# A sliding-window copy from DRAM to DRAM: row by row in 64 KB packets, or in four orders of addresses

## The chip, the cores and the metric

One core of one Trainium2 chip runs the kernel. The metric is the device time of one launch in microseconds (us), lower is better. Before the change the median of two runs is 819.74 us (819.61 and 819.86).

## What is computed

The input `x` has 32 batches of 4096 rows of 256 float32 values. A window is 64 rows and starts every 32 rows, so each batch has 127 windows, and every window is copied out whole:

```python
def reference(x, window_size, stride):          # 64, 32
    batch, length, dim = x.shape                # 32, 4096, 256
    n_windows = (length - window_size) // stride + 1        # 127
    result = np.zeros((batch, n_windows, window_size, dim), dtype=np.float32)
    for i in range(n_windows):
        start = i * stride
        result[:, i] = x[:, start:start + window_size].copy()
    return result
```

A window is 64 x 256 x 4 = 65,536 bytes, contiguous in the input and in the output. Two neighbouring windows share half of their input. Below, a "block" is half a window: 32 rows, 32 KB. A batch of the input is 128 blocks (4 MiB, exactly 2^22 bytes); every block but the first and the last of a batch stands in the output twice, as the second half of one window and as the first half of the next. The output has 32 x 127 = 4064 windows, 266.34 MB.

## The kernel before, in words

Nothing is computed, and no data passes through on-chip memory: each DMA reads DRAM and writes DRAM. `STRATEGY` is "d2d", so the kernel runs `_d2d`, which goes through the 32 batches and calls `_d2d_batch` for each, always on the SyncE queue (`D2D_NQ = 1`). The other strategies of the file are never called. `_d2d_batch` issues two DMAs a batch (line 26): one of 112 windows (`D2D_CHUNK`) and one of the 15 that remain. The input side of both is an overlapping view of rows, the output side is plain:

```python
src = bass.AP(x.tensor, x.offset + (b * L + w0 * S) * D,
              [[step_elems, nw], [1, win_elems]])      # 32 KB apart, 64 KB long
dst = out_flat[b * n_win + w0 : b * n_win + w0 + nw]
q.dma_start(out=dst, in_=src, max_dma_last_dim=65536)
```

One row is one packet of 64 KB. A DMA is dealt out over the core's 16 DMA engines by its outer dimension. The 112 rows go seven to an engine; the 15 go one to an engine and leave one engine out. So over the whole kernel 15 engines get 32 x 8 = 256 rows each and one gets 32 x 7 = 224.

The order is that of the loop. The scheduling layer gives the DMAs eight semaphores in turn and makes SyncE wait, ahead of each DMA from the ninth on, until the DMA eight places earlier has landed; so at most eight DMAs (four batches) are in flight. The kernel ends when SyncE has seen the last ones land (line 297).

Of the kernel before, what the change touches and what calls it, by code (L numbers as in the profile page):

```python
# [7 lines left out]
STRATEGY = "d2d"  # L8
NSB = 7

D2D_CHUNK = 112


def _d2d_batch(q, x, out_flat, b, L, D, W, S, n_win):
    win_elems = W * D
    step_elems = S * D
    w0 = 0
    while w0 < n_win:
        nw = min(D2D_CHUNK, n_win - w0)
        src = bass.AP(  # L20
            x.tensor,
            x.offset + (b * L + w0 * S) * D,
            [[step_elems, nw], [1, win_elems]],
        )
        dst = out_flat[b * n_win + w0 : b * n_win + w0 + nw]
        q.dma_start(out=dst, in_=src, max_dma_last_dim=65536)
        w0 += nw


D2D_NQ = 1  # L30


def _d2d(nc, x, out, B, L, D, W, S, n_win):
    out_flat = out.rearrange("b i w d -> (b i) (w d)")
    queues = [nc.sync, nc.scalar][:D2D_NQ]
    for b in range(B):
        _d2d_batch(queues[b % len(queues)], x, out_flat, b, L, D, W, S, n_win)


class _SbufBatch:  # L40

    def __init__(self, tc, ctx, x, out, B, L, D, W, S, n_win, bufs=3):
        assert W % S == 0 and L % S == 0
        self.m = W // S
        self.n_blocks = L // S
        assert self.n_blocks <= 128
        self.blk = S * D
        self.n_win = n_win
        self.x_blocks = x.rearrange("b (n s) d -> b n (s d)", n=self.n_blocks)
        self.out_rows = out.rearrange("b i w d -> b i (w d)")  # L50
        self.pool = ctx.enter_context(tc.tile_pool(name="swin_sbuf", bufs=bufs))
        self.dtype = x.dtype
        self.chunks = []
        w0 = 0
        for cnt in (64, 48, 16, 15):
            while n_win - w0 >= cnt or (w0 < n_win and cnt == 15):
                cnt_eff = min(cnt, n_win - w0)
                self.chunks.append((w0, cnt_eff))
                w0 += cnt_eff
        assert sum(c for _, c in self.chunks) == n_win  # L60

    def alloc(self):
        return self.pool.tile([self.n_blocks, self.blk], self.dtype, name="xb")

    def load(self, q, t, b):
        q.dma_start(out=t[:, :], in_=self.x_blocks[b])

    def stores(self, q, t, b):
        for k in range(self.m):
            for (w0, cnt) in self.chunks:  # L70
                src = t[w0 + k : w0 + k + cnt]
                dst = self.out_rows[b, w0 : w0 + cnt, k * self.blk : (k + 1) * self.blk]
                q.dma_start(out=dst, in_=src, max_dma_last_dim=65536)


def _sbuf(ctx, tc, nc, x, out, B, L, D, W, S, n_win):
    sb = _SbufBatch(tc, ctx, x, out, B, L, D, W, S, n_win, bufs=4)
    queues = [nc.sync, nc.scalar]
    tiles = {}
    for b in range(B):  # L80
        t = sb.alloc()
        tiles[b] = t
        sb.load(queues[b % 2], t, b)
        if b >= 1:
            sb.stores(queues[(b - 1) % 2], tiles[b - 1], b - 1)
            del tiles[b - 1]
    sb.stores(queues[(B - 1) % 2], tiles[B - 1], B - 1)


def _mix(ctx, tc, nc, x, out, B, L, D, W, S, n_win, nsb=None, lookahead=2):  # L90
    if nsb is None:
        nsb = NSB
    out_flat = out.rearrange("b i w d -> (b i) (w d)")
    sb = _SbufBatch(tc, ctx, x, out, B, L, D, W, S, n_win, bufs=4)
    queues = [nc.sync, nc.scalar]

    span = B - 4
    sbuf_set = set()
    if nsb > 0:
        for j in range(nsb):  # L100
            sbuf_set.add(1 + j * span // nsb)
    assert len(sbuf_set) == nsb

    def flush_stores(qidx):
        t, bb = pending.pop(0)
        j = 0
        for (w0, cnt) in sb.chunks:
            for k in range(sb.m):
                q = queues[(qidx + j) % 2]
                src = t[w0 + k : w0 + k + cnt]  # L110
                dst = sb.out_rows[bb, w0 : w0 + cnt, k * sb.blk : (k + 1) * sb.blk]
                q.dma_start(out=dst, in_=src, max_dma_last_dim=65536)
                j += 1

    pending = []
    n_d2d_left = B - nsb
    for b in range(B):
        q = queues[b % 2]
        if b in sbuf_set:
            t = sb.alloc()  # L120
            sb.load(q, t, b)
            pending.append((t, b))
            if len(pending) > lookahead:
                flush_stores(b % 2)
        else:
            _d2d_batch(q, x, out_flat, b, L, D, W, S, n_win)
            n_d2d_left -= 1
            if pending and n_d2d_left < 2 * len(pending):
                flush_stores(b % 2)
    qi = 0  # L130
    while pending:
        flush_stores(qi)
        qi += 1


def _pair(ctx, tc, nc, x, out, B, L, D, W, S, n_win, nsb=None):
    if nsb is None:
        nsb = NSB
    assert 3 * nsb + 4 <= B - nsb, "not enough d2d batches to pair"
    out_flat = out.rearrange("b i w d -> (b i) (w d)")  # L140
    sb = _SbufBatch(tc, ctx, x, out, B, L, D, W, S, n_win, bufs=4)
    queues = [nc.sync, nc.scalar]
    blk = sb.blk

    sbuf_batches = [4 * g for g in range(nsb)]
    d2d_batches = [b for b in range(B) if b not in set(sbuf_batches)]
    di = 0

    W_CHUNKS = [(0, 64), (64, 48), (112, 15)]
    L_CHUNKS = [(0, 64), (64, 48), (112, 16)]  # L150

    def d2d_chunk(q, b, w0, cnt):
        src = bass.AP(
            x.tensor,
            x.offset + (b * L + w0 * S) * D,
            [[S * D, cnt], [1, W * D]],
        )
        q.dma_start(
            out=out_flat[b * n_win + w0 : b * n_win + w0 + cnt],
            in_=src,  # L160
            max_dma_last_dim=65536,
        )

    def load_part(q, t, b, p0, cnt):
        q.dma_start(out=t[p0 : p0 + cnt], in_=sb.x_blocks[b, p0 : p0 + cnt])

    def store_part(q, t, b, w0, cnt, k):
        src = t[w0 + k : w0 + k + cnt]
        dst = sb.out_rows[b, w0 : w0 + cnt, k * blk : (k + 1) * blk]
        q.dma_start(out=dst, in_=src, max_dma_last_dim=65536)  # L170

    tiles = {}
    n_groups = nsb + 2
    for g in range(n_groups):
        qa = queues[g % 2]
        qb = queues[1 - g % 2]
        a_instrs = []
        if g < nsb:
            bload = sbuf_batches[g]
            t = sb.alloc()  # L180
            tiles[bload] = t
            for (p0, cnt) in L_CHUNKS:
                a_instrs.append(("load", t, bload, p0, cnt, None))
        if g >= 2:
            bst = sbuf_batches[g - 2]
            ts = tiles.pop(bst)
            for (w0, cnt) in W_CHUNKS:
                for k in range(sb.m):
                    a_instrs.append(("store", ts, bst, w0, cnt, k))
        b_needed = [ins[4] for ins in a_instrs]  # L190
        b_instrs = []
        nb_d2d = 3 if g < nsb else 2
        for _ in range(nb_d2d):
            bd = d2d_batches[di]
            di += 1
            for (w0, cnt) in W_CHUNKS:
                b_instrs.append((bd, w0, cnt))
        n = max(len(a_instrs), len(b_instrs))
        for i in range(n):
            if i < len(a_instrs):  # L200
                ins = a_instrs[i]
                if ins[0] == "load":
                    load_part(qa, ins[1], ins[2], ins[3], ins[4])
                else:
                    store_part(qa, ins[1], ins[2], ins[3], ins[4], ins[5])
            if i < len(b_instrs):
                bd, w0, cnt = b_instrs[i]
                d2d_chunk(qb, bd, w0, cnt)
    rem = d2d_batches[di:]
    for j, bd in enumerate(rem):  # L210
        for (w0, cnt) in W_CHUNKS:
            d2d_chunk(queues[j % 2], bd, w0, cnt)


def _hybrid(ctx, tc, nc, x, out, B, L, D, W, S, n_win):
    out_flat = out.rearrange("b i w d -> (b i) (w d)")
    sb = _SbufBatch(tc, ctx, x, out, B, L, D, W, S, n_win, bufs=3)

    sbuf_batches = [b for b in range(B) if (b + 1) * NSB // B > b * NSB // B]
# [16 lines left out]
    if pending is not None:  # L236
        sb.stores(q_sb, pending[0], pending[1])
# [64 lines left out]
```

## Time and profile before

| What | Value |
|---|---|
| median of the runs | 819.74 us |
| span of the profiled execution, first to last instruction | 805.2 us |
| the profiled execution's own time outside the span | not recorded; the median lies 14.5 us above the span |
| DMAs issued, all by SyncE | 64 |
| data packets of 64 KB | 4064 |
| 4-byte packets (semaphore updates) | 992 |
| bytes read, bytes written | 266.34 MB each |
| share of the span in which the packets' time fills the 16 engines | 98.3% |
| mean rate over the span | 331 GB/s read, and as much written |

Apart from four short fills of constants on GpSimd at the start, no compute engine does anything. The page's row "DMA" gives the busy share of the 16 DMA engines in 40 slices of the span, the row "GB/s" what they moved (counted once, though each byte is read and written). The same two numbers can be asked of any stretch of the span. Besides these, the trace holds start, duration and size of every single packet, without its address and without the engine's number; packets that follow each other end to start can be strung into sixteen sequences, one for each engine, nearly without a gap.

### The profile page before, as it was taken

How to read it: one execution, taken by the hardware profiler on the slowest of the kernel's cores; microseconds unless marked ns; L12 is line 12 of the kernel's file. 1: busy time of each engine (PE TensorE's matmuls, PEld its weight loads, DVE VectorE, ACT ScalarE, POOL GpSimd, SP SyncE). 2: the span in 40 equal slices, each digit the busy share in tenths (PEclk: the TensorE clock that was granted, in tenths of full speed). 3: DMA queues.
4: the chain of work that ended last, by engine and by line, in shares of the span. 5: the costliest groups of instructions: out<-in, count | busy, mean ns of one | idle time of the engine just before them, and what ended most of it. 6: DMA issues, size and time to landing. Idle time of an engine off the chain costs nothing. (4 is left out here: it accounts for less than half of the span.)

```text
span 805.2 us, 109 instructions
## 1 busy us (share of the span) xinstructions
POOL 0.2 (0%) x4
## 2 busy tenths in 40 slices
POOL 0000000000000000000000000000000000000000
DMA  9999999999999999999999999999999999999995
GB/s 313 355 322 332 342 316 352 322 339 335 319 358 313 322 352 319 348 329 335 339 316 358 319 329 348 313 361 319 335 335 332 342 322 339 332 322 332 326 335 254
DMA packets 5056, 266.34 MB, mean 331 GB/s; under 512 B 992, under 2 KB 992, under 8 KB 992
## 3 DMA queue, kind: packets, MB, share of 16 engines
q1 hardware_dynamic: 5056, 266.34, 98.3%
HBM read 266.34 MB, written 266.34 MB: 662 GB/s over the span
## 5 line engine op out<-in xcount | busy, mean ns | idle before, releaser
L283 POOL MEMSET const-bfloat16-1.0<- 128x1 bf16 x1 | 0.1, 101 | 0.0
L283 POOL MEMSET const-uint8-127<- 128x1 uint8 x1 | 0.1, 101 | 0.0
L283 POOL MEMSET const-float32-0.0<- 128x1 f32 x1 | 0.1, 98 | 0.2 <-issue 0.2
L283 POOL MEMSET const-float32-1.0<- 128x1 f32 x1 | 0.1, 98 | 0.0
## 6 DMA issues: line engine op xcount, KB each, us to landing
out_dram<-in_x_dram SPq DMA_DIRECT2D x64, 100.5
```

The costliest lines, as they stand in the source:

```text
L283: nc = _bacc.Bacc("TRN2", target_bir_lowering=False, num_devices=1)
```

## The change

The strategies are removed, and with them the scheduling layer's part: a class issues the DMAs on SyncE inside a critical section, all on one semaphore, and SyncE waits once, at the end, for the sum of all increments. The copy is cut into four parts, issued in this order:

1. `batch_each`: the first 63 windows of batches 0 to 15, in one DMA. Its outer dimension is the batch, so that each engine gets a batch: 63 rows of 64 KB, one after the other. The sources of two engines lie 4 MiB apart, their targets 127 x 64 KB.
2. `side_by_side`: the last 64 windows of batches 0 to 15, one DMA a batch. The outer dimension steps by one window, so the 16 engines copy 16 neighbouring windows, then the next 16: four rows of 64 KB for each engine.
3. `both_places` with one piece, batches 16 to 23: the source is a block, named twice by a step of 0; the target is the two places of this block, which lie side by side (64 KB) in the output. A packet is 32 KB. One DMA has 112 blocks, one has 14; the first and the last block of the batch, which have one place, are a DMA each of 16 packets of 2 KB.
4. The same with eight pieces, batches 24 to 31: each block is cut into eight pieces of 4 KB, and a DMA copies the same piece of 112 (or 14) blocks to both places. The packets are 4 KB; a batch has eighteen DMAs.

The bytes read and written are the same as before.

```diff
-STRATEGY = "d2d"
-NSB = 7
-
-D2D_CHUNK = 112
+PIECES = 8
...
-        q.dma_start(out=dst, in_=src, max_dma_last_dim=65536)
...
+class _Copies:
+    def __init__(self, engine, sem, x, out, W, S):
+        self.engine, self.sem, self.x, self.out = engine, sem, x, out
+        self.B, self.L, self.D = x.shape
+        self.blk, self.win = S * self.D, W * self.D
+        self.n_blk = self.L // S
+        self.n_win = self.n_blk - 1
+        self.total = 0
...
+    def start(self, b, block, src, half, dst, packet):
+        x_at = self.x.offset + (b * self.n_blk + block) * self.blk
+        out_at = self.out.offset + b * self.n_win * self.win + half * self.blk
+        self.engine.dma_start(
+            out=bass.AP(self.out.tensor, out_at, dst),
+            in_=bass.AP(self.x.tensor, x_at, src),
+            max_dma_last_dim=4 * packet,
+        ).then_inc(self.sem, 16)
+        self.total += 16
+
+    def batch_each(self, b0, w0, n):
+        src = [[self.n_blk * self.blk, 16], [self.blk, n], [1, self.win]]
+        dst = [[self.n_win * self.win, 16], [self.win, n], [1, self.win]]
+        self.start(b0, w0, src, 2 * w0, dst, self.win)
+
+    def side_by_side(self, b, w0, n):
+        src = [[self.blk, 16], [16 * self.blk, n // 16], [1, self.win]]
+        dst = [[self.win, 16], [16 * self.win, n // 16], [1, self.win]]
+        self.start(b, w0, src, 2 * w0, dst, self.win)
+
+    def both_places(self, b, pieces):
+        n = self.blk // pieces
+        for p0, count in ((1, 112), (113, self.n_blk - 114)):
+            for c in range(pieces):
+                x_at = self.x.offset + (b * self.n_blk + p0) * self.blk + c * n
+                out_at = self.out.offset + b * self.n_win * self.win + (2 * p0 - 1) * self.blk + c * n
+                src = bass.AP(self.x.tensor, x_at, [[self.blk, count], [0, 2], [1, n]])
+                dst = bass.AP(self.out.tensor, out_at, [[self.win, count], [self.blk, 2], [1, n]])
+                self.engine.dma_start(out=dst, in_=src, max_dma_last_dim=4 * n).then_inc(self.sem, 16)
+                self.total += 16
+        end = [[self.blk // 16, 16], [1, self.blk // 16]]
+        self.start(b, 0, end, 0, end, self.win)
+        self.start(b, self.n_blk - 1, end, 2 * self.n_win - 1, end, self.win)
...
-    if STRATEGY == "d2d":
-        _d2d(nc, x, out, B, L, D, W, S, n_win)
...
+    with tc.tile_critical():
+        sem = nc.alloc_semaphore("copied")
+        c = _Copies(nc.sync, sem, x, out, int(window_size), int(stride))
+        rest = c.n_win - 64
+        c.batch_each(0, 0, rest)
+        for b in range(16):
+            c.side_by_side(b, rest, 64)
+        for b in range(16, 24):
+            c.both_places(b, 1)
+        for b in range(24, c.B):
+            c.both_places(b, PIECES)
+        nc.sync.wait_ge(sem, c.total)
+        nc.sync.sem_clear(sem)
```

In the built program SyncE issues 1 + 16 + 8 x 4 + 8 x 18 = 193 DMAs in place of 64. Two neighbouring targets of `both_places` are merged on the output side, which then reads 224 (or 28) runs; its slowest dimension and the source's (112, or 14) are divided over 16 engines, or over 14.

More of the change, by code (lines that the diff above doesn't have):

```diff
@@ L6 @@
 from concourse._compat import with_exitstack
-STRATEGY = "d2d"
-NSB = 7
-D2D_CHUNK = 112
[L14 to L27, printed above, removed]
@@ L30 @@
[L30 to L73, printed above, removed]
@@ L76, in _sbuf @@
[L76 to L133, printed above, removed]
@@ L136, in _pair @@
[L136 to L212, printed above, removed]
@@ L215, in _hybrid @@
[L215 to L219, printed above, removed]
-    d2d_batches = [b for b in range(B) if b not in set(sbuf_batches)]
-    q_d2d = nc.sync
-    q_sb = nc.scalar
-    pending = None
-    prefetch = None
-    for b in range(B):
-        if b in set(d2d_batches):
-            _d2d_batch(q_d2d, x, out_flat, b, L, D, W, S, n_win)
-        else:
-            t = sb.alloc()
-            sb.load(q_sb, t, b)
-            if pending is not None:
-                sb.stores(q_sb, pending[0], pending[1])
-            pending = (t, b)
-    if pending is not None:
-        sb.stores(q_sb, pending[0], pending[1])
+PIECES = 8
@@ new lines @@
+class _Copies:
[6 more added lines that the diff above has]
+        self.total = 0
+        assert W == 2 * S and (self.L - W) // S + 1 == self.n_win == 127
+    def start(self, b, block, src, half, dst, packet):
[28 more added lines that the diff above has]
+        self.start(b, self.n_blk - 1, end, 2 * self.n_win - 1, end, self.win)
@@ L249 @@
     nc = tc.nc
-    W = int(window_size)
-    S = int(stride)
-    B, L, D = x.shape
-    n_win = (L - W) // S + 1
-    assert out.shape == (B, n_win, W, D), (out.shape, (B, n_win, W, D))
-    if STRATEGY == "d2d":
-        _d2d(nc, x, out, B, L, D, W, S, n_win)
-    elif STRATEGY == "sbuf":
-        _sbuf(ctx, tc, nc, x, out, B, L, D, W, S, n_win)
-    elif STRATEGY == "mix":
-        _mix(ctx, tc, nc, x, out, B, L, D, W, S, n_win)
-    elif STRATEGY == "pair":
-        _pair(ctx, tc, nc, x, out, B, L, D, W, S, n_win)
-    else:
-        _hybrid(ctx, tc, nc, x, out, B, L, D, W, S, n_win)
+    with tc.tile_critical():
[11 more added lines that the diff above has]
+        nc.sync.sem_clear(sem)
 _INS = ['x', 'window_size', 'stride']
```

## Prediction

> **What bounds the kernel now.** I read the page first. Its first line and the parts on DMA leave no other candidate: no compute engine works, and one queue fills the 16 DMA engines for 98.3% of the span.
>
> ```profile
> span 805.2 us, 109 instructions
> ...
> DMA packets 5056, 266.34 MB, mean 331 GB/s; under 512 B 992, under 2 KB 992, under 8 KB 992
> ## 3 DMA queue, kind: packets, MB, share of 16 engines
> q1 hardware_dynamic: 5056, 266.34, 98.3%
> HBM read 266.34 MB, written 266.34 MB: 662 GB/s over the span
> ...
> out_dram<-in_x_dram SPq DMA_DIRECT2D x64, 100.5
> ```
>
> 5056 packets are 4064 rows of 64 KB and 992 semaphore updates. A DMA lands 100.5 us after its issue in the median, so the queue is always deep. Whether SyncE ever holds the engines up is in the waits of the DMA queue and in the row of line 26:
>
> ```profile
> SPq L26 <- DMA out_dram<-in_x_dram: 662.8, 56, 21.6
> ...
> L26 SPq DMA_DIRECT2D out_dram<-in_x_dram x64: 528/748/927, 0.7 to 707.6; - x64
> ```
>
> It does not: an issue takes 528 to 927 ns, a batch needs two, and SyncE spends 662.8 us waiting for room. A busy engine is not yet an engine at its peak, so the third view is the table by stretches (length, GpSimd, clock, DMA share, GB/s):
>
> ```profile
> 5.00:400.00 395.00, 0.00 (x0) 1.00 1.00 333
> 400.00:720.00 320.00, 0.00 (x0) 1.00 1.00 333
> 740.00:780.00 40.00, 0.00 (x0) 1.00 0.95 333
> 780.00:800.00 20.00, 0.00 (x0) 1.00 0.77 315
> 800.00:805.20 5.20, 0.00 (x0) 1.00 0.23 101
> ```
>
> Divide the rate by the share and by 16 for the speed of a working engine: 333/16 = 20.8 GB/s while all work, 315/(0.77 x 16) = 25.6 when a quarter has finished, 101/(0.23 x 16) = 27.4 at the end. An engine alone could do 27; sixteen together are held to 333 GB/s, and with 95% of the share the sum is still 333. So the bound is shared: not the engines, but the path to the memory or the memory itself. The packet records say the same. In the steady part (3407 packets) a 64 KB packet takes 3.138 us in the mean, 2.418 at the least, 2.801 and 3.485 at the tenth and ninetieth percentile, 3.874 at the ninety-ninth, 5.127 at the most. When the engine with 224 rows has finished, some 75 us before the end, three others go to 2.42 us at once, while the other twelve stay at 3.1 to 3.2; when those three finish, the twelve go to 2.418. A packet starts within 5 ns of the end of the one before it, 2 ns with a 4-byte update between.
>
> A second thing in these records matters here: the engines keep in step. After 256 packets each, the last twelve engines finish between 801.3 and 804.1 us, less than one packet apart.
>
> The sum of the profiled execution: 2.2 us to the first packet, 801.9 of packets, 1.2 to the last instruction, 805.2. The median of the runs is 819.74; the 14.5 us outside the span I carry over unchanged.
>
> **The change part by part.** At 333 GB/s the four parts would take: 1008 windows, 66.06 MB, 198.4 us; 1024 windows, 67.11 MB, 201.5 us; twice 1016 windows, 66.58 MB, 200.0 us. Sum 799.9, against 801.9 of packets now; 2 us are the ragged end.
>
> *The waits of SyncE, the issues.* 56 waits go, one comes at the very end; nothing stands behind it but the clearing of the semaphore. 193 issues replace 64. 72 of them, on 14 engines, I price by the upper row of line 26 (820 ns, which the 15-window DMAs show), 121 by the lower (528): 59.0 + 63.9 = 123 us over a span of 800, beside the transfers. The tightest place is part 4: 18 issues a batch, 8 x 0.82 + 10 x 0.53 = 11.9 us, against 25 us of transfer. Cost 0. The cover is gone if an issue takes more than 25/18 = 1.39 us there. The first packet can't be earlier, as the first issue is at the same place.
>
> *The balance.* Parts 1 and 2 give each engine 63 + 64 = 127 rows, where 15 engines had 128 and one 112. Parts 3 and 4 give 14 engines eight rows' worth a batch and two of them seven. Under a shared bound the uneven engine cost little (333 GB/s at 95%), so evening it saves at most the 2 us of the end, and the new unevenness (16 rows fewer on two engines) gives about as much back. Cost 0, between -2 and +2.
>
> *Updates and small packets.* An engine gets up to 193 semaphore updates for 63; at 9 ns a packet that is +1.2 us, and 32 packets of 2 KB. Both lie under the shared bound. Cost 0, at most +2.
>
> *Part 2, rows side by side.* 64 KB packets; neighbouring engines read 32 KB apart and write 64 KB apart, where the present sources are 7 x 32 KB apart and the targets 7 x 64 KB (seven rows to an engine). It is the nearest to the present order: 3.138 us a packet, cost 0. The bounds are 64 x (2.801 - 3.138) = -22 and 64 x (3.485 - 3.138) = +22 us, if all went like the tenth or the ninetieth percentile.
>
> *Part 3, a block to both places.* The distances are the present ones, and packets are half as long; a packet follows the last one within 5 ns, so twice as many of them cost nothing under a bound of 333. Cost 0, with the same bounds of -22 and +22.
>
> *Part 4, 4 KB packets.* 8 x 128 = 1024 packets an engine. The share of the bound is 3.138/16 = 196 ns a packet; the engine alone needs 2.418/16 = 151 and, with the 9 ns of an update's packet as its fixed cost, 160. That is hidden: cost 0. The other end: the next smaller packets that the trace has are instruction fetches of 8 KB, 361 ns at the least. If a 4 KB packet took that, it would be 1024 x (0.361 - 0.196) = +169 us. They are single transfers with nothing behind them, so the row of 64 KB, where packets follow without a gap, is nearer.
>
> *Part 1, a batch to each engine.* This is the part that I expect to cost. Its 16 sources lie 4 MiB apart, a power of two, and all start at the same place of a batch. As the engines keep in step to within a packet, they stay near the same place of their batches for the whole part. Whatever the low bits of an address choose on the path to memory, all sixteen reads choose alike, where now they stand seven blocks apart. The targets are spread (127 x 64 KB). The trace has no such row. Ends: 63 packets at 2.418 us give 63 x (2.418 - 3.138) = -45 us; at 5.127 us, the worst single packet, +125 us. I take the ninetieth percentile, a packet that now meets bad company one time in ten: 63 x (3.485 - 3.138) = +22 us. The engines are elastic: whoever is held back falls behind and leaves the crowd, so I do not go to the worst.
>
> Here the Trainium skill, "DMA: Bandwidth & Descriptors", section "Latency and other measured facts", speaks against the change: copies whose rows lie 4 MiB apart in memory ran at 103 GB/s each way where a pitch of 512 KiB gave 207 and a padded one 214. By that ratio as an estimate part 1 would take 198 x 214/103 = 412 us and the kernel about 1033. No row of this trace shows such a pitch; the page's rows were 16 KB and both sides were pitched, here they are 64 KB and the reads alone.
>
> Sum: 805.2 + 22 = 827 us of span, and 14.5: **842 us**.
>
> **Rivals.**
>
> A, the forecast: part 1 is held back, by +17 to +125 us (3.40 to 5.13 us a packet), the time 836 to 945. For it: the steps in unison and the shared bound. Against it: a packet of 64 KB walks through many addresses, and a lag of a few kilobytes may be enough to part the streams.
>
> B, the order does not matter: all parts run at 333 GB/s, 818 to 823 us, with small gains and losses 808 to 836. For it: 333 GB/s hardly changes over the whole span, and 662 GB/s read and written looks like one ceiling for the sum of all traffic. Its place is part 1: it decides as long as the mean packet there stays under 3.138 + 16.4/63 = 3.40 us. This is the "not slower" side.
>
> C, small packets: part 4 needs more than 196 ns a packet. It passes 2% at 1024 x 16 ns = +16.4, that is from 212 ns; at 361 ns the time is 989. Besides a fixed cost, a reason would be the addresses: the pieces of one DMA are all the same 4 KB of every 32 KB. Against it: the gapless packets, and the 45 ns between 196 and 151.
>
> D, faster: the present order itself costs rate, and parts 2 and 3 take the tenth percentile, -22 us each, 776 to 803. Against it: with a quarter of the engines done, the rate does not rise above 333.
>
> That the change does not do what it says (an engine's share dealt otherwise than by the outer dimension) would turn part 1 into the present order, and so into B; it is counted there.
>
> **How the numbers follow.** A 0.42, B 0.38, C 0.15, D 0.05. A is the likeliest; its own range is 836 to 945, and its point 842 for the mild end that I argued for. A range for 8 in 10 has to hold B and most of A and C: 812 to 925 leaves out D (0.05), the top of A (0.04) and of C (0.08). About 2%, 16.4 us, is what a measurement of this kernel can tell from no change. Faster 0.05 (D), within 2% 0.38 (B), slower 0.57 (A and C).
>
> **What would show it.** The rate in the stretches: part 1 from 2 to about 220 us at about 300 GB/s (66.06 MB in 220 us), the rest at 333. The mean 64 KB packet of the first 1008: near 3.49 us if A, near 3.14 if B. The 4 KB packets at the end: near 196 ns with a DMA share near 1.00 if they are hidden. SyncE issues everything early or waits for room; if DMA shares fall under 0.9 in part 4 while SyncE issues without a pause, the issues were the bound. I am wrong if the first 220 us run at 333, or if the loss sits in part 4.

## The result, and the profile after

The kernel after takes 1013.25 us in the median of two runs (1011.83 and 1014.67), the kernel before 819.74. The ratio is 1.2365, with a 95% interval of 1.232 to 1.241. The forecast was 842 us in a range of 812 to 925: the direction was right, the size was not.

The page of the kernel after, its head and its DMA rows:

```profile
span 1012.9 us, 240 instructions
...
DMA  9999999999999999999999999999999999999997
GB/s 166 166 173 181 171 158 186 160 171 166 166 166 166 166 186 251 316 324 331 331 331 331 329 318 324 318 321 330 326 326 319 322 323 324 326 328 320 326 320 256
DMA packets 23633, 266.36 MB, mean 263 GB/s; under 512 B 2944, under 2 KB 2944, under 8 KB 19584
```

The row "DMA" looks as it did before: full throughout. Only the row under it shows the loss. Fifteen slices of 25 us move 158 to 186 GB/s. Part 1 ends in the sixteenth, and those that follow move 316 to 331, but for the last one (256). The engines count as busy either way. The table by stretches of the kernel after (length, GpSimd, clock, DMA share, GB/s) puts the parts beside each other: part 1 in the first two rows, then parts 2, 3 and 4, then the end:

```profile
0.00:200.00 200.00, 0.20 (x4) 1.00 0.99 168
200.00:380.00 180.00, 0.00 (x0) 1.00 1.01 172
400.00:590.00 190.00, 0.00 (x0) 1.00 1.00 327
600.00:780.00 180.00, 0.00 (x0) 1.00 1.00 324
800.00:1000.00 200.00, 0.00 (x0) 1.00 1.00 323
1000.00:1012.90 12.90, 0.00 (x0) 1.00 0.52 195
```

Part 1 runs at half the rate, evenly from start to end. In the packet records its 1008 packets of 64 KB take 6.173 us in the mean (5.19 and 7.13 at the tenth and ninetieth percentile), where a packet of before took 3.138. That is 63 x (6.173 - 3.138) = +191 us an engine. The rest, 200.28 MB, runs at about 325 instead of 333 GB/s: 616 against 601 us, +15. The sum, 206, is the growth of the span (1012.9 - 805.2 = 207.7) to within 2 us. The two medians lie only 193.5 us apart, because the profiled execution of before was quicker than the two runs shown (see the last item on the prediction). So a part of the +15 is that execution's rate: the first experiment, which undoes part 1 alone, leaves 8 us.

SyncE hardly waits on a semaphore any more. The two lines that issue, of the kernel after:

```profile
L28 SPq DMA_DIRECT2D out_dram<-in_x_dram x49: 570/1802/49707, 1.0 to 999.7; - x49
...
L57 SPq DMA_DIRECT2D out_dram<-in_x_dram x144: 588/847/35197, 409.5 to 998.2; - x144
```

An issue now takes up to 49.7 us. The waiting for room has moved from the semaphores into the issue itself; it is the same room, and shares of 0.99 to 1.01 in all four parts show that the engines did not lack work.

### The profile page after: what moved, and what is told of

Same layout as the page of the kernel before. It is cut to its first block, busy times and chain, and to the rows that moved or that the text cites. A ratio compares the mean times of both kernels' runs of the same rounds, so it can differ in the third digit from the quotient of the medians.

```text
span 1012.9 us, 240 instructions
## 1 busy us (share of the span) xinstructions
POOL 0.2 (0%) x4
```

## The experiments

Two theories stood after the result. The first: the sources of part 1, 4 MiB apart and walked in step, collide. The rivals: its targets, the walk of one engine through one batch, or the new way of issuing.

**Part 1 alone undone** (`e1_part1_side_by_side`).

```diff
-        c.batch_each(0, 0, rest)
+        for b in range(16):
+            c.side_by_side(b, 0, 48)
+            c.plain(b, 48, 15)
```

> The kernel after with part 1 alone undone: windows 0 to 62 of batches 0 to 15 go as 48 rows side by side and 15 plain rows, a DMA each, in place of the batch for each engine; all else stays. Theory (the whole loss sits in part 1's addresses): the time falls by about 190 us, to 820 to 832, the rate in the first 200 us rises from 169 to about 330 GB/s. Rival (the new way of issuing, small packets or unevenness cost too): it stays over 840.

825.1 us against 817.14 for the kernel before on the same chip: ratio 1.0089 (1.0066 to 1.0112). The loss was part 1's, but for this 0.9%.

**Which side collides** (`e2_which_side`). In this kernel and the two that follow, `rows` starts a copy with a pitch and a step (in KB) for the source and for the target, and waits for it.

```diff
+        c.rows(4096, 32, 127 * 64, 64)
+        c.rows(4096, 32, 64, 1024)
+        c.rows(32, 512, 127 * 64, 64)
+        c.rows(32, 512, 4096, 64)
+        c.rows(32, 512, 64, 1024)
```

> Only 16 x 32 rows of 64 KB (33.55 MB) are copied, five times in turn, each copy awaited before the next; most of the output is left out and part of it goes to other places. Five address patterns, sources and targets of neighbouring engines apart by: (a) 4 MiB and 127 x 64 KB, as in part 1; (b) 4 MiB and 64 KB; (c) 32 KB and 127 x 64 KB; (d) 32 KB and 4 MiB; (e) 32 KB and 64 KB. Theory (reads at a pitch of 4 MiB collide): a and b take about 200 us (169 GB/s), c and e about 101 us (333), and d shows whether writes at 4 MiB collide too: about 200 if the collision is in the memory's layout, 101 if it is in the reads alone. Rival 1 (the targets of part 1 are to blame): a and c slow, b fast. Rival 2 (an engine that walks alone through a batch, and reads each half twice, is slow whatever the pitch): a, b and also c, d unlike e.

The stretches, one from the middle of each of the five copies a to e:

```profile
10.00:180.00 170.00, 0.00 (x0) 1.00 1.00 178
200.00:370.00 170.00, 0.00 (x0) 1.00 1.00 177
390.00:480.00 90.00, 0.00 (x0) 1.00 1.01 333
500.00:680.00 180.00, 0.00 (x0) 1.00 1.00 168
700.00:785.00 85.00, 0.00 (x0) 1.00 0.99 326
```

a and b are slow alike, c is not: part 1's targets are innocent, its sources are to blame. d shows that the side does not matter as such: targets 4 MiB apart halve the rate too, with sources that are spread. Rival 2 is not decided here, since only a and b walk through consecutive sources; the next experiment does it.

**How far apart is enough** (`e3_stagger`): sources 4 MiB plus a stagger apart.

```diff
+        c.rows(4096 + 0, 32, 64, 1024)
+        c.rows(4096 + 1, 32, 64, 1024)
+        c.rows(4096 + 4, 32, 64, 1024)
+        c.rows(4096 + 16, 32, 64, 1024)
+        c.rows(4096 + 32, 32, 64, 1024)
+        c.rows(4096 + 64, 32, 64, 1024)
+        c.rows(4096 + 128, 32, 64, 1024)
```

> Seven copies in turn of 16 x 32 rows of 64 KB, each awaited before the next, the targets always 64 KB apart; most of the output is left out, and the data of the staggered copies are shifted. The sources are 4 MiB apart plus a stagger of 0, 1, 4, 16, 32, 64 and 128 KB from engine to engine. Theory (the same place of a batch at the same time is what collides): stagger 0 takes about 200 us, and from some stagger on it is 101 us; which one tells how large the piece of memory is that they fight for. Rival (a distance of some 4 MiB costs whatever the place, as by more memory pages in use at once): all seven take about 200 us.

The seven copies in order:

```profile
10.00:180.00 170.00, 0.00 (x0) 1.00 0.98 176
200.00:370.00 170.00, 0.00 (x0) 1.00 0.99 179
390.00:540.00 150.00, 0.00 (x0) 1.00 1.00 205
555.00:650.00 95.00, 0.00 (x0) 1.00 0.98 300
665.00:760.00 95.00, 0.00 (x0) 1.00 1.01 320
775.00:865.00 90.00, 0.00 (x0) 1.00 1.00 326
880.00:970.00 90.00, 0.00 (x0) 1.00 1.00 326
```

A stagger of 1 KB changes next to nothing, 4 KB little, 16 KB most, 64 KB the rest. It is no switch: the rate rises with the distance between neighbours. And as the walk of each engine is the same in all seven, rival 2 of the last experiment is out.

**Which pitches** (`e4_pitch`).

```diff
+        c.rows(224, 32, 64, 1024)
+        c.rows(512, 32, 64, 1024)
+        c.rows(1024, 32, 64, 1024)
+        c.rows(2048, 32, 64, 1024)
+        c.rows(4096, 32, 64, 1024)
+        c.rows(8192, 32, 64, 1024)
```

> Six copies in turn of 16 x 32 rows of 64 KB, each awaited, targets 64 KB apart; most of the output is left out and data go to other places. The sources are 224 KB (as in the kernel before), 512 KB, 1, 2, 4 and 8 MiB apart. Theory (address bits above some place do not choose the piece of memory): fast (101 us) up to a pitch, then slower by steps, 4 and 8 MiB about 200 us. Rival (any power of two collides): 512 KB is slow already.

```profile
10.00:100.00 90.00, 0.00 (x0) 1.00 1.00 326
115.00:205.00 90.00, 0.00 (x0) 1.00 0.99 315
225.00:315.00 90.00, 0.00 (x0) 1.00 1.00 307
335.00:450.00 115.00, 0.00 (x0) 1.00 1.00 255
470.00:640.00 170.00, 0.00 (x0) 1.00 0.99 177
660.00:830.00 170.00, 0.00 (x0) 1.00 1.00 182
```

224 KB, the kernel before, is free; 512 KB costs 3%, 1 MiB 6%, 2 MiB 22%, 4 and 8 MiB about 45%. So a distance of 4 or 8 MiB works as if it were none, and a power of two alone is not the trouble.

**One way alone, first attempt** (`e5_one_way`), through on-chip memory on 16 partitions at a time.

```diff
+        for store, pitch, step in ((0, 32, 512), (0, 4096, 32), (1, 64, 1024), (1, 4096, 64)):
...
+            for i in range(24):
+                here = t[16 * (i // 3) : 16 * (i // 3) + 16, 16384 * (i % 3) : 16384 * (i % 3 + 1)]
+                there = bass.AP(tensor.tensor, tensor.offset + i * step * kb, [[pitch * kb, 16], [1, 16384]])
```

> Four transfers in turn of 24 x 16 rows of 64 KB (25.17 MB) between DRAM and on-chip memory, each awaited; no window is copied as such, and nearly all of the output is left out. (a) loads, sources 32 KB apart; (b) loads, sources 4 MiB apart; (c) stores, targets 64 KB apart; (d) stores, targets 4 MiB apart. With nothing in the way the 16 engines move 16 x 27.1 = 434 GB/s: 58 us. Theory 1 (the ceiling of 333 GB/s each way is the sum of reads and writes at the memory; a pitch of 4 MiB lowers the memory's own limit): a and c run near 420 to 434 GB/s; b and d run well under them, near 200 to 350, as one way alone now bears the whole collision. Theory 2 (reads and writes are slowed only where they meet, as in turning between them): b and d run as fast as a and c.

Inconclusive: the loads ran at 110 GB/s and the stores at 127, the spread ones too (a load's packet of 64 KB took 9.5 us). So the distance in DRAM was not the bound here; the on-chip side, 16 partitions at a time, is the likely one, which no run shows by itself.

**The remedy inside the kernel** (`e6_staggered`): still a batch for each engine, started at different windows.

```diff
+    def batch_each_staggered(self, n, s):
+        src = [[self.n_blk * self.blk + s * self.blk, 16], [self.blk, n], [1, self.win]]
+        dst = [[self.n_win * self.win + s * self.win, 16], [self.win, n], [1, self.win]]
+        self.start(0, 0, src, 0, dst, self.win)
...
-        c.batch_each(0, 0, rest)
+        c.batch_each_staggered(rest, 4)
         for b in range(16):
-            c.side_by_side(b, rest, 64)
+            c.in_pieces(b, 0, 4 * b)
+            c.in_pieces(b, 4 * b + rest, 64 - 4 * b)
```

> The kernel after with part 1 moved: engine e starts its batch at window 4e, so that neighbours' sources are 4 MiB + 128 KB apart (targets 127 x 64 KB + 256 KB); the windows left over in batches 0 to 15 (64 in each) replace part 2 and are copied in 4 KB packets, a sixteenth of a window for each engine. The whole output is written. Theory (the same place at the same time): as fast as with part 1 undone, 820 to 830 us, though still a batch for each engine. Rival (a batch for each engine costs as such): over 900.

828.24 us against 817.5 on the same chip, ratio 1.0126 (1.0095 to 1.0158). Its part 1:

```profile
5.00:200.00 195.00, 0.00 (x0) 1.00 1.01 331
```

331 GB/s, where the same walk without the stagger had 168 to 172, and where the order of before has 329 and 330 on this chip (next run). The order "a batch for each engine" costs nothing, the common starting place was what cost.

**The order of before, issued as after** (`e7_before_order_free`).

```diff
+        for b in range(c.B):
+            c.plain(b, 0, 112)
+            c.plain(b, 112, 15)
```

> The kernel before's 64 DMAs in its order, issued as the kernel after issues them: one semaphore, one wait at the end, no wait between. Theory (the new way of issuing costs nothing): 815 to 819 us, as the kernel before on the same chip; then the 0.9% that stayed with part 1 undone lies in parts 2 to 4 and their end. Rival (an ungated queue lets the engines drift apart and costs some rate): 822 to 828 us, the whole of the rest.

817.01 us, ratio 0.9992 (0.9981 to 1.0003): the way of issuing costs nothing. What stayed in the first experiment lies in the rate of its parts: its stretches run at 322 to 328, this kernel's at 329 and 330 (on another chip, where the kernel before takes 817.5 against 817.14). Why they are a per cent or two slower was not followed further.

**Fewer reads, more to carry** (`e8_mix7`).

```diff
-STRATEGY = "d2d"
+STRATEGY = "mix"
```

> The kernel before with its own other strategy: seven of the 32 batches are loaded into on-chip memory once and stored twice, the others go as before, on two queues. Reads fall by 7 x 4.13 MB = 29 MB of 266, while the engines carry 29.4 MB more. If the ceiling is the sum of reads and writes (about 660 GB/s), the time falls by 29/660 = 44 us to about 775. If it is the 333 GB/s that the engines carry of any copy, it rises by 29.4/333 = 88 us to about 905. If writes alone are the ceiling (266 MB whatever the reads), it stays at about 817.

851.01 us, ratio 1.0393 (1.0344 to 1.0442), none of the three. Its engines carry 295.70 MB at a mean of 348 GB/s, more than 333, while reads and writes together fall to 592 GB/s. Neither simple ceiling holds, and the kernel changes too much at once (queues, on-chip side) to tell more.

**One way alone, over all partitions** (`e9_one_way_all_rows`).

```diff
+        for store, pitch, step in ((0, 16, 2048), (0, 1024, 16), (1, 16, 2048), (1, 1024, 16)):
...
+                here = t[:, 4096 * i : 4096 * (i + 1)]
+                there = bass.AP(tensor.tensor, tensor.offset + i * step * kb, [[pitch * kb, 128], [1, 4096]])
```

> Four transfers in turn of 12 x 128 rows of 16 KB (25.17 MB) between DRAM and on-chip memory, each awaited, now over all 128 partitions; no window is copied as such, and nearly all of the output is left out. (a) loads, rows 16 KB apart; (b) loads, rows 1 MiB apart, so that the engines, four rows from each other, are at the same place modulo 4 MiB; (c), (d) the same for stores. Theory (in one and the same place the memory gives some 178 GB/s, whichever way): a and c 400 to 434 GB/s (58 to 63 us), b and d 178 to 200 (126 to 141 us). Theory 2 (the place bears some 356 GB/s in sum of reads and writes, half of which was the other way in the copies): b and d about 350 (72 us). Theory 3 (only reads and writes together collide): b and d as a and c.

```profile
5.00:60.00 55.00, 0.00 (x0) 1.00 1.01 429
66.00:124.00 58.00, 0.00 (x0) 1.00 1.01 415
130.00:185.00 55.00, 0.00 (x0) 1.00 1.00 424
190.00:246.00 56.00, 0.00 (x0) 1.00 1.01 423
```

Loads and stores at the colliding distance run near the engines' own speed. For the stores this is a test in step: in the packet records of copy d the engines' packets of the same number end within 0.17 us of each other up to the seventeenth (a packet takes 0.61 us), and in this stretch the rate is full:

```profile
189.00:199.00 10.00, 0.00 (x0) 1.00 1.01 424
```

For the loads it is not: in copy b the packets of the same number end 1.2 to 2.7 us apart from the start, two to four rows, and these lie 1 MiB from each other. So for stores my theory of a place with a fixed capacity falls, in its half-way form too, and theory 3 is left; for loads this run decides nothing.

**Fewer engines** (`e10_fewer_engines`): `rows` on 4, 8 and 12 engines.

```diff
+        c.rows(32, 512, 64, 1024, k=4)
+        c.rows(4096, 32, 64, 1024, k=4)
+        c.rows(32, 512, 64, 1024, k=8)
+        c.rows(4096, 32, 64, 1024, k=8)
+        c.rows(32, 512, 64, 1024, k=12)
+        c.rows(4096, 32, 64, 1024, k=12)
```

> Six copies in turn, on 4, 8 and 12 engines of the 16, 32 rows of 64 KB on each, first with sources 32 KB apart, then 4 MiB apart, targets 64 KB apart, each awaited; most of the output is left out. Apart, the engines run at their own 27.1 GB/s: 108, 217 and 325. Theory (one place has a fixed capacity of about 178 GB/s): in step 108, 178 and 178. Rival (each pair of streams costs, a slowdown in proportion to their number): 4 engines are slow already, under 90, and 12 engines do better than 16 with over 200.

```profile
10.00:70.00 60.00, 0.00 (x0) 1.00 0.25 109
90.00:150.00 60.00, 0.00 (x0) 1.00 0.25 109
170.00:235.00 65.00, 0.00 (x0) 1.00 0.50 218
250.00:315.00 65.00, 0.00 (x0) 1.00 0.49 213
330.00:395.00 65.00, 0.00 (x0) 1.00 0.76 327
410.00:500.00 90.00, 0.00 (x0) 1.00 0.71 245
```

Neither expectation held whole: the theory's 178 was passed by eight and by twelve, and of the rival only the last part came, over 200 with twelve. Four engines lose nothing, eight 2%, twelve 25%, and sixteen (177 in the copies above) do less in sum than eight. Eight streams alone in one place pass nearly free. The 245 of twelve is not one rate; a stretch near its start and one near its end:

```profile
410.00:430.00 20.00, 0.00 (x0) 1.00 0.73 210
460.00:480.00 20.00, 0.00 (x0) 1.00 0.74 262
```

By the packet records the twelve start together, and their third to fifth packets take 3.8 to 4.1 us in the mean, some 200 GB/s in sum. Then four draw ahead and end at 491 to 492 us, while the other eight end at 508 to 509. So engines can leave the crowd; with sixteen they did not (see the part on the prediction). Nor are two crowds of eight free side by side: at the pitch of 2 MiB above, where every second engine is in the same place, sixteen engines had 255 of 326.

**Apart in time, not in address** (`e11_lag_in_time`): a lead-in is to give each engine two rows more than the next, then all walk with sources exactly 4 MiB apart.

```diff
+    def lead_in(self):
+        for k in range(15, 0, -1):
+            for again in range(2):
...
+        c.lead_in()
+        c.rows(4096, 32, 64, 1024, 63)
```

> A copy of 16 x 63 rows of 64 KB with sources 4 MiB apart, targets 64 KB apart, as in part 1, but ahead of it engine e copies other rows first, two more than engine e + 1 (28 on engines 0 and 1, none on engine 15), so that the engines walk the same addresses modulo 4 MiB one after the other, two rows apart, instead of together. Most of the output is left out. Theory (the same place at the same time): while all are on the walk it runs near 326 GB/s; the whole, 82 MB, takes about 260 us. Rival (the addresses alone count, at whatever time): the walk runs near 177 GB/s, and the whole takes over 400 us. Between: they start apart and fall into step again, since an engine that is ahead meets no one and one behind catches up only if it is faster.

```profile
90.00:230.00 140.00, 0.00 (x0) 1.00 1.00 312
230.00:240.00 10.00, 0.00 (x0) 1.00 0.85 282
```

312 GB/s for 140 us with sources at the very pitch that gives 177 when all walk together. The lag was not quite the planned one. SyncE issued the walk only 24.3 us in, when the engines with the shortest lead-ins were through: by the packet records six engines end their walk together, at 239 to 241 us, and the other ten after them, up to 287.5 us, mostly 4 to 7 us from one to the next. The six together cost little, in line with the eight of the run before. Those that start apart stay apart. The whole span was 288.8 us, longer than the 260 I expected, because the engines with most rows finish late.

**One way, in the same walk as part 1** (`e12_one_way_same_walk`), **and with a control that is dealt alike** (`e13_one_way_control`). The edit is shown against the run `e9_one_way_all_rows`.

```diff
-                ... [[pitch * kb, 128], [1, 4096]]
+                ... [[pitch * kb, 16], [4096, 8], [1, 4096]]
```

> Four transfers in turn of 12 x 16 x 128 KB (25.17 MB) between DRAM and on-chip memory, each awaited; no window is copied as such, and nearly all of the output is left out. (a) loads, engines 128 KB apart; (b) loads, engines 4 MiB apart, each walking through consecutive addresses as in part 1; (c), (d) the same for stores. It closes a gap of the run before, whose rows jumped by 1 MiB within an engine. Theory (one way alone does not collide, as the 419 and 402 GB/s of the last loads say): b as a, d as c. Rival (the walk in step collides one way too, and the jumping rows hid it): b near 178 to 250 GB/s, d alike, whatever a and c are.

> Five transfers in turn of 12 x 16 x 128 KB (25.17 MB), as in the run before, with a control that is dealt to the engines in the same way: (a) loads, engines 160 KB apart; (b) loads, 4 MiB apart; (c) loads, 4 MiB + 128 KB apart; (d) stores, 160 KB apart; (e) stores, 4 MiB apart. The 217 GB/s of the loads at 4 MiB is just half of 433, which the on-chip side could cause too, by two engines on one way in. If the memory is the cause: a and c 400 to 430 GB/s, b 217. If the on-chip side is: a, b and c all near 217, and then the one-way question stays open for loads. For stores: d 425 throughout; e starts near 250 and comes free, as before, if that was the memory, and d does so too if it was the on-chip side.

In the first of the two the loads 4 MiB apart ran at 219 GB/s and their control at 429. That looks like a collision. The second, its loads 160 KB, 4 MiB and 4 MiB + 128 KB apart, then the start and the end of its stores 160 KB apart, and the start and the end of its stores 4 MiB apart:

```profile
20.00:110.00 90.00, 0.00 (x0) 1.00 1.01 214
125.00:235.00 110.00, 0.00 (x0) 1.00 1.01 219
245.00:355.00 110.00, 0.00 (x0) 1.00 1.01 213
365.00:380.00 15.00, 0.00 (x0) 1.00 0.98 265
400.00:425.00 25.00, 0.00 (x0) 1.00 1.01 429
438.00:452.00 14.00, 0.00 (x0) 1.00 1.00 261
480.00:500.00 20.00, 0.00 (x0) 1.00 1.01 429
```

All loads are at 213 to 219, the spread ones too, so the distance is not the cause. The on-chip side is what is left; the first control, 128 KB apart and so one contiguous stretch of memory, had presumably been dealt otherwise. For loads this shows no collision up to 219 GB/s, with the engines in step (packets of the same number end within 1.8 us of each other in the first of the two runs). Whether loads alone collide above that, no run shows.

The stores 4 MiB apart took as long as the spread ones, 71.8 us each by the packet records, after the same slow start at 261 and 265 GB/s. At 429 they were no longer in step: by the fiftieth packet the engines stood up to 6 us apart, some ten packets. So in this walk stores in step show no collision up to 261 GB/s, far over the 168 that they had in the copy; at the full rate the run `e9_one_way_all_rows` shows it, at 424.

## Why the prediction was wrong, step by step

- *The bound.* Right: a shared limit of the path to memory or the memory, not the engines. That limit was then not the constant of 333 for which I took it, but depends on where the streams stand.
- *Issues, waits, semaphore.* Right: 0.9992 for the order of before without any wait, and a DMA share of 1.00 in part 4, where the issues stand closest.
- *Part 4, 4 KB packets.* Right: 201 ns in the mean against 196, at a DMA share of 1.00, in a part that runs at 323 GB/s. The fixed cost is hidden; rival C did not occur.
- *Parts 2 and 3.* Right to 2 or 3%: 327 and 324 GB/s against 333, a 64 KB packet of part 2 at 3.194 us against 3.138.
- *Part 1.* The place and the mechanism were right: all sources at the same place of their batches, at the same time. The stagger in address and the lag in time both bear it out. The failed step is the size, "63 x (3.485 - 3.138) = +22", for which the runs put +191, and the sentence that carried it: "The engines are elastic: whoever is held back falls behind and leaves the crowd". In the packet records of part 1 the 1008 ends fall into 63 rounds of sixteen, and no round overlaps the next. The sixteen ends of a round lie 2.4 us apart in the median from first to last, 3.7 at the most; their standard deviation is 0.7 us in the fifth round and 0.5 in the sixtieth. Nobody leaves. In 2.4 us an engine moves 26 KB at 10.6 GB/s. Spread over sixteen engines, that is under 2 KB from neighbour to neighbour as an estimate, and the staggered copies still ran at 179 GB/s with 1 KB and at 205 with 4 KB. The sentence is not wrong of every crowd: of twelve engines, four did leave. I had myself noted that the engines keep in step and then argued against it.
- *The choice of the row.* The ninetieth percentile of packets that meet by chance says nothing about packets that meet always. The worst single packet, 5.127 us, was taken as the end of the range; the mean in part 1 lies above it.
- *The page.* By the Trainium skill's figure ("DMA: Bandwidth & Descriptors", "Latency and other measured facts"), rows 4 MiB apart at 103 of 214 GB/s, the estimate was 1033 us. Measured were 1013 us, and in part 1 169 GB/s (66.06 MB in 390 us): 333/169 = 1.97 where the page's figures give 2.08. I set the page aside because rows and sides differed; here that made little difference to the size. The page also says that 4 KiB more on the row pitch restored the full rate. The distance from engine to engine is another measure: there 4 KB gave 205 GB/s, and it took 64.
- *The 14.5 us.* They were no overhead. The after run of 1014.67 us has a span of 1012.9, so 1.8 lie outside, and the kernel before has about 2 outside on the other chips (817.5 with a span of 815.4). So the profiled execution of before was some 12 us quicker than the two runs shown; the kernel before's medians lie between 805.5 and 819.7 us over all chips used here. This was worth 1.5% of the base and did not decide.

Rival B failed where it said: the mean packet of part 1 passed 3.40 us.

## What to carry to other kernels

When sixteen engines are dealt a large outer dimension each, look at the pitch: sixteen streams that start together 4 or 8 MiB apart stay together and halve a DRAM-to-DRAM copy, and the profile shows nothing but full engines at half the rate. Shift neighbours by 64 KB or start them apart, and the same order is free or nearly so. And when a trace shows that streams run in step, price a collision as lasting, not as an accident.

## What was not expected of the hardware

- The collision was seen in copies only: one with its reads in step had 177 GB/s and one with its writes in step 168, though the other side was spread. Stores alone in step ran at 424. Loads alone in step ran at 219, where the spread ones were held as well, so for loads a collision at higher rates is not excluded. What in the memory makes reads and writes meet so is not settled.
- It sets in between eight and twelve streams (213 of 218 GB/s with eight, 245 of 327 with twelve), and sixteen move less in sum than eight (177).
- Sixteen engines in step stay in step under the collision, for all 63 rounds of part 1; of twelve, four drew ahead. Engines that start apart stay apart, at 312 GB/s.
- Packet size, from 64 KB down to 4 KB, and reading a block twice in a row made no difference of more than 2% between parts 2, 3 and 4 (327, 324 and 323 GB/s).
